# A chunked recurrence inside a decoder layer: its output products take other places in the chunk

## The chip, the cores and the metric

One NeuronCore of one Trainium2 chip runs the whole kernel as one program. The metric is device time in microseconds (us), the median over several executions. The profile is one further execution under the hardware profiler, with its own time.

## What is computed

The reference is one decoder layer over 512 tokens and 1024 channels in float32: two parallel token mixers (an RWKV-7 recurrence with 16 heads of 64, and a three-branch sparse attention), a gated merge, and a gated MLP. The change is inside the recurrence, which per head is

```python
def step(state, inp):
    r_t, w_t, k_t, v_t, a_t, b_t = inp
    sa = jnp.einsum('bhvk,bhk->bhv', state, a_t)
    state = (state * w_t[:, :, None, :] + sa[..., None] * b_t[:, :, None, :]
             + v_t[..., None] * k_t[:, :, None, :])
    return state, jnp.einsum('bhvk,bhk->bhv', state, r_t)
```

run over the 512 tokens. Its results y are normalised per head, scaled by a gate and projected later.

## The kernel before, in words

The kernel does not step token by token. It cuts the 512 tokens into 8 chunks of 64 and works on 8 heads at once: a group has GP = 4 pairs of heads, and there are two groups, so the recurrence runs twice, once per group. Heads of a pair are named h = 0, 1 and lie in partitions 0 to 63 and 64 to 127; pairs of a group are named i.

Per group and chunk c the function `recur` (lines 666 to 798) does the following, each product being of 64 by 64 outputs:

1. xw (lines 760 to 763), for c > 0: the old state St against part 0 of AR. 8 products with 64 rows of contraction, shape 64x64 on TensorE. They go to columns 0 to 255 of the PSUM bank `xw`.
2. W (line 765): VectorE adds LV to xw. GpSimd prepares the decayed state SD meanwhile (line 770).
3. `outputs` of the chunk before (lines 721 to 736, called at 774), explained below.
4. TT (lines 775 to 778): TT times W, 8 products of shape 64x64, to columns 256 to 511 of `xw` and `xs`. VectorE (line 779) and ScalarE (line 780) copy the two halves to UV.
5. A `yield`, then xs (lines 784 to 787): 8 products of BKT with UV, 128 rows of contraction and 64 output partitions, shape 128x64. Line 791 (793 for c = 0) adds SD and gives the next state. Another `yield`.

`outputs(c)` computes y for chunk c: "carried" products of part 1 of AR with the state at the chunk's start (lines 727 to 730, shape 64x64, 8 products, none for c = 0), and "inner" products of GS with UV (lines 731 to 733, shape 128x64, 8 products) that add to the same PSUM sums. It is called one chunk late, between W and TT of chunk c + 1. Its order is by quarters: four carried, four inner, four carried, four inner. In each (head, pair) the carried product opens the sum with start=True and the inner product closes it. The sums live in two PSUM banks `y`, one for each h; one half of the columns of a bank holds two chunks, an even and an odd one, in opposite halves of the partitions. After an odd chunk ScalarE copies the finished half bank to YT (line 736, one instruction for each h). The two banks are allocated anew at c = 0 and c = 4, from a tag with two buffers, so chunk 4 takes over the banks of chunks 0 to 3.

In chunks 3 to 7 the statistics of finished chunk pairs run beside this (`stat1`, `stat2`, lines 741 to 750): a sum on VectorE (743), a scaling (744), a subtraction on GpSimd (745), a square on ScalarE (747), a second sum on VectorE (750).

What fills the waits: a driver interleaves this generator with projection steps (`proj_steps`, lines 286 to 293, each step three 128x512 matmuls at lines 290 to 292 with a shape of 128x128). About one such step is placed in program order at each `yield`. A list scheduler then builds the queues: an instruction that is ready goes by its place in the program, and one that is not ready lets later ones pass. Engines run their queues in order. In the first group the fill is the gate projections and the inputs of head pair 4 (`r`, `v` in the profile), then the preparation of pair 4 (`prep`, lines 495 to 557); in the second it is the query projections (`q`).

After the first group come `finish` (lines 800 to 844) and the preparation of the second group's four pairs; after the second come `finish` again and the attention, whose tables `dist`, `cdist` and `cmask` (lines 945 to 950) are loaded into memory that the recurrence has freed.

Of the kernel before, what the change touches and what calls it, by code (L numbers as in the profile page):

```python
# [32 lines left out]
GP = 4  # L33
# [9 lines left out]
def hybrid_layer(ctx: ExitStack, tc: tile.TileContext, a, out, dbg=None, stop=None):  # L43
    nc = tc.nc
    te, ve, sc, po, sy = nc.tensor, nc.vector, nc.scalar, nc.gpsimd, nc.sync
# [15 lines left out]
    def px(name):  # L61
        return ps.tile([128, 512], F32, tag="px", name=name, bufs=2)

    def py(name):
        return ps.tile([128, 512], F32, tag="py", name=name, bufs=2)
# [63 lines left out]
    def evict(i):  # L129
        last[i.ins.engine] = i  # L130
        return i

    def behind(i):
        tc.add_manual_dep(i.ins, last[i.ins.engine].ins.name,
                          mybir.DependencyInfo(mybir.DependencyClass.NoSync, mybir.DependencyReason.DATA),
                          reason="behind the last eviction")
        return i
# [528 lines left out]
    def recur(gr, g):  # L666
        x1 = gr.x1
        TT = gr.TT
        XN = x1[:, 0].rearrange("p c u -> p u c")
        M2 = x1[:, 0].rearrange("p (i c) t -> p i c t", c=8)  # L670
        L2 = x1[:, 1].rearrange("p (i c) t -> p i c t", c=8)
        yield
        gi = "p (i c j) -> p i c j"
        for q in range(GP // 2):
            pt = px(f"mt{g}{q}")
            ptv = pt.rearrange(gi, i=2, j=32)
            for i in range(2):
                for c in range(8):
                    for h in range(2):
                        lo, up = slice(64 * h, 64 * h + 32), slice(64 * h + 32, 64 * h + 64)  # L680
                        m = te.matmul(ptv[up, i, c], L2[lo, 2 * q + i, c], XN[lo, 16 * q + 8 * i + c], start=True,
                                      stop=True)
                        if q + i + c + h == 0:
                            tc.keep_in_program_order(m)
                yield
                yield
            for h in range(2):
                up = slice(64 * h + 32, 64 * h + 64)
                if h == 0:
                    act_m = sc.activation(M2[up, 2 * q:2 * q + 2], ptv[up], AF.Copy)  # L690
                else:
                    ve.tensor_copy(M2[up, 2 * q:2 * q + 2], ptv[up])
        evict(act_m)
        for h in range(2):
            lo = slice(64 * h, 64 * h + 32)
            behind(sc.activation(gr.diag[0][lo, :, 0:32], gr.diag[1][lo], AF.Copy))
        yield
        for q in range(GP // 2):
            pm = px(f"mm{g}{q}")
            pmv = pm.rearrange(gi, i=2, j=32)  # L700
            for i in range(2):
                for c in range(8):
                    for h in range(2):
                        lo, up = slice(64 * h, 64 * h + 32), slice(64 * h + 32, 64 * h + 64)
                        te.matmul(pmv[lo, i, c], M2[up, 2 * q + i, c], TT[up, 2 * q + i, c, 32:64], start=True,
                                  stop=True)
                yield
                yield
            for h in range(2):
                lo = slice(64 * h, 64 * h + 32)  # L710
                if h == 0:
                    sc.activation(TT[lo, 2 * q:2 * q + 2, :, 32:64], pmv[lo], AF.Copy)
                else:
                    ve.tensor_copy(TT[lo, 2 * q:2 * q + 2, :, 32:64], pmv[lo])
        YT = gr.YT = rh_.tile([128, 4, GP, 2, 64], F32, tag="XB", name=f"YT{g}", bufs=2)
        yield
        hs = [slice(0, 64), slice(64, 128)]
        iv = "p (i v) -> p i v"
        yps = [None]

        def outputs(c, Sc):
            if c % 4 == 0:
                yps[0] = [py(f"y{g}{c}{h}").rearrange("p (a i v) -> p a i v", i=GP, v=64) for h in range(2)]
            y = [b[:, c // 2 % 2] for b in yps[0]]
            for q in range(GP // 2):
                four = [(0, 2 * q), (1, 2 * q + 1), (0, 2 * q + 1), (1, 2 * q)]
                if c:
                    for h, i in four:
                        te.matmul(y[h][hs[(c + i) % 2], i], gr.AR[i][hs[h], 1, c * 64:(c + 1) * 64], Sc[hs[h], i],
                                  start=True, stop=False)  # L730
                for h, i in sorted(four):
                    te.matmul(y[h][hs[(c + i) % 2], i], gr.GS[:, 1 + i, c, h, :], gr.UV[:, c, i, h, :],
                              start=c == 0, stop=True)
            if c % 2:
                for h in range(2):
                    sc.activation(YT[:, c // 2, :, h], y[h], AF.Copy)

        st = gr.st = rh_.tile([128, 2, 4, 2 * GP], F32, tag="gst", name=f"gst{g}", bufs=1)
        sq = gr.sq = {}

        def stat1(a, keep):
            Y8 = YT[:, a].rearrange("p i h v -> p (i h) v")
            keep(ve.tensor_reduce(st[:, 0, a], Y8, axis=AX.X, op=OP.add))
            ve.tensor_scalar(st[:, 0, a], st[:, 0, a], 1.0 / 64, None, op0=OP.mult)
            po.tensor_tensor(Y8, Y8, st[:, 0, a, :, None].to_broadcast([128, 2 * GP, 64]), op=OP.subtract)
            sq[a] = rh_.tile([128, 2 * GP, 64], F32, tag="TB", name=f"SQ{g}{a}", bufs=1)
            sc.activation(sq[a], Y8, AF.Square)

        def stat2(a, keep):
            keep(ve.tensor_reduce(st[:, 1, a], sq[a], axis=AX.X, op=OP.add))  # L750

        def free(i):
            return i

        St = None
        prev = None
        for c in range(8):
            xw, xs = px(f"xw{g}{c}"), px(f"xs{g}{c}")
            if c:
                for i in range(GP):  # L760
                    for h in range(2):
                        te.matmul(xw[hs[h], i * 64:i * 64 + 64], gr.AR[i][hs[h], 0, c * 64:(c + 1) * 64],
                                  St[hs[h], i], start=True, stop=True)
                W = rh_.tile([128, GP, 64], F32, tag="W", name=f"W{g}{c}", bufs=1)
                ve.tensor_tensor(W, xw[:, 0:64 * GP].rearrange(iv, v=64), gr.LV[:, :, c, :], op=OP.add)
                if c >= 3:
                    (stat2 if c % 2 == 0 else stat1)((c - 3) // 2, tc.keep_in_program_order)
                if c < 7:
                    SD = rh_.tile([128, GP, 64], F32, tag="SD", name=f"SD{g}{c}", bufs=1)
                    po.tensor_tensor(SD, St, gr.Dc[:, :, c, None].to_broadcast([128, GP, 64]), op=OP.mult)  # L770
            else:
                W = gr.LV[:, :, 0, :]
            if prev:
                outputs(*prev)
            for i in range(GP):
                for h in range(2):
                    te.matmul((xw, xs)[h][0:64, 256 + i * 64:320 + i * 64], TT[hs[h], i, c, :], W[hs[h], i], start=True,
                              stop=True)
            ve.tensor_copy(gr.UV[0:64, c, :, 0, :], xw[0:64, 256:512].rearrange(iv, v=64))
            sc.activation(gr.UV[0:64, c, :, 1, :], xs[0:64, 256:512].rearrange(iv, v=64), AF.Copy)  # L780
            yield
            prev = c, St
            if c < 7:
                for i in range(GP):
                    for h in range(2):
                        te.matmul(xs[hs[h], i * 64:i * 64 + 64], gr.BKT[i][:, c, hs[h]], gr.UV[:, c, i, h, :],
                                  start=True, stop=True)
                SN = rh_.tile([128, GP, 64], F32, tag="S", name=f"S{g}{c + 1}", bufs=2)
                xsv = xs[:, 0:64 * GP].rearrange(iv, v=64)
                if c:  # L790
                    ve.tensor_tensor(SN, xsv, SD, op=OP.add)
                else:
                    ve.tensor_copy(SN, xsv)
                St = SN
                yield
        outputs(*prev)
        stat2(2, free)
        stat1(3, free)

# [57 lines left out]
    def core(g):  # L857
        return spawn(invert(G[g], g), 0, 1.0), spawn(recur(G[g], g), RD[g], RR[g])
# [646 lines left out]
```

## Time and profile before

| what | value |
|---|---|
| median of 3 runs | 1210.08 us (1209.62 to 1210.79) |
| profiled execution, its time | 1209.59 us |
| profiled execution, span first to last instruction | 1207.8 us |
| TensorE busy | 1174.6 us |
| VectorE, ScalarE, GpSimd busy | 584.6, 582.8, 587.8 us |
| first recurrence, first TT product to last y product | 248.66 to 284.48 us |
| second recurrence | 466.54 to 503.85 us |

In the lines of a profile PE is TensorE's matmul side, PEld its weight loads, DVE is VectorE, ACT ScalarE, POOL GpSimd, and SP the engine that issues most DMAs. A line of the timeline gives start, duration, engine, source line, operation, output<-inputs, the operand form (contraction*output partitions, then the moving operand), a count, and in brackets the idle time before it and what ended it. Each float32 product of the recurrence is two matmul instructions in the trace, so 8 products show as x16. Matmuls overlap in the array, so what a block of them costs is read from the difference between its start and the start of what follows, not from the durations.

### The profile page before, as it was taken

The numbers are of one execution on the slowest core, as the hardware profiler recorded it, in microseconds if no ns is written. First come the engines' busy times: TensorE is split into PE (matmuls) and PEld (weight loads), VectorE is DVE, ScalarE is ACT, GpSimd is POOL, SyncE is SP. The second block draws the span as 40 slices with busy tenths as digits, with TensorE's granted clock in tenths as the row PEclk, the third lists the DMA queues.
The fourth block names the chain that finished last, engine by engine and source line by source line (L and its number), as shares of the span: only waits on it lengthen the run. The fifth ranks groups of instructions, "written<-read, shape, count | busy, mean of one in ns | idle before, by whom it ended". The sixth has DMA issues, their size and how long they took to land.

```text
span 1207.8 us, 19849 instructions
## 1 busy us (share of the span) xinstructions
PE 1174.6 (97%) x7414; PEld 934.0 (77%) x7414; DVE 584.6 (48%) x1196; ACT 582.8 (48%) x1141; POOL 587.8 (49%) x529
## 2 busy tenths in 40 slices
PE   8999999999999999989999999999999999999997
PEld 6888878777777887767666666888888888888886
DVE  4226555436465463476687774855343333431103
ACT  5446653436565334476665664544444444443311
POOL 4336654344565443465466652531366555554440
PEclk8999999999899999999999999999999999999999
DMA  6522335310343543345332214761133333334421
GB/s 220 136 73 81 92 94 166 124 50 22 104 119 103 157 141 115 109 149 184 105 105 71 71 46 127 229 212 37 50 98 92 101 96 97 96 97 131 132 70 70
DMA packets 95651, 131.95 MB, mean 109 GB/s; under 512 B 34177, under 2 KB 37057, under 8 KB 95298
## 3 DMA queue, kind: packets, MB, share of 16 engines
q1 hardware_dynamic: 79634, 116.26, 32.0%
q10 hardware_dynamic: 15920, 14.42, 3.7%
q8 instruction: 58, 0.95, 0.3%
q14 instruction: 39, 0.32, 0.1%
HBM read 108.30 MB, written 19.14 MB: 106 GB/s over the span
## 4 chain that ended last, share of the span: by engine, by line
PE 82%; DVE 7%; ACT 3%; issue 3%; POOL 2%; DMA 2%; SPq 0%; DVEq 0%; POOLq 0%; ACTq 0%
PE pu L212 6%; PE pu L213 6%; PE pu L214 6%; PE dn L1238 3%; PE dn L1236 3%; PE dn L1237 3%; PE o L1080 3%; PE pt L140 3%; PE ub L1132 2%; PE ub L1133 2%; PE ub L1134 2%; PE v L290 2%; PE v L292 2%; PE v L291 2%; PE gt L292 2%
## 5 line engine op out<-in xcount | busy, mean ns | idle before, releaser
L1051 ACT ACTIVATE p<-p,stt 128x384 f32<-128x384 f32 (+3 forms) x128 | 70.9, 555 | 55.7 <-DVE stt L1049 55.4
L1027 POOL TENSOR_SCALAR p<-p,stt 128x512 f32<-128x512 f32 (+1 forms) x64 | 74.1, 1167 | 33.5 <-DVE stt L1022 24.8
L1376 DVE SCALAR_TENSOR_TENSOR u<-pu,cvec,u 128x511 f32<-128x511 f32 x44 | 33.0, 750 | 101.7 <-ACT u L1375 101.7
L1049 DVE CUSTOM_DVE_ANT_0 p<-s,rh 128x384 f32<-128x384 f32 (+3 forms) x128 | 58.4, 484 | 27.9 <-PE s L1044 18.8
L1080 PE MATMUL o<-PT,vt 128*64 128x384 f32 (+3 forms) x256 | 50.5, 451 | 1.1 <-DVE PT L1101 1.1
L140 PE MATMUL pt<-ident,p 128*128 128x128 f32 x320 | 49.6, 276 | 0.0
L1380 POOL TENSOR_TENSOR u<-u,u 128x512 f32<-128x512 f32 x22 | 28.3, 1288 | 38.3 <-DVE u L1377 37.4
L140 PEld LDWEIGHTS pt<-ident,p 128*128 128x128 f32 x320 | 40.1, 142 | 8.4 <-issue 0.4
L1382 DVE TENSOR_TENSOR al<-u,ah 128x512 fp32r<-128x512 f32 x22 | 23.8, 1080 | 45.4 <-ACT ah L1381 45.4
L1044 PE MATMUL s<-kst,qs 128*128 128x512 f32 (+1 forms) x128 | 37.5, 392 | 1.4 <-DVE stt L1049 1.0
L1375 ACT ACTIVATE u<-pu,cvec 128x512 f32<-128x512 f32 x44 | 33.6, 764 | 5.0 <-PE pu L1340 5.0
L1027 DVE TENSOR_SCALAR p<-p,stt 128x512 f32<-128x512 f32 (+1 forms) x64 | 35.0, 581 | 0.9
L1099 ACT ACTIVATE PT<-pt 128x512 f32<-128x512 f32 x48 | 27.9, 582 | 13.5 <-PE pt L140 11.3
L1377 DVE SCALAR_TENSOR_TENSOR u<-pu,cvec,u 128x510 f32<-128x510 f32 x44 | 32.9, 749 | 1.6
L1080 PEld LDWEIGHTS o<-PT,vt 128*64 128x64 f32 x256 | 16.7, 136 | 20.2 <-issue 14.5
L1101 DVE COPY PT<-pt 128x512 f32<-128x512 f32 x32 | 22.0, 686 | 19.2 <-PE pt L140 19.1
L1044 PEld LDWEIGHTS s<-kst,qs 128*128 128x128 f32 x128 | 23.0, 193 | 8.2 <-DVE stt L1049 2.7
L1284 DVE TENSOR_TENSOR p2tm<-dn,gb 128x512 f32<-128x512 f32 x4 | 2.8, 692 | 51.2 <-ACT p2jl L1282 51.2
L587 PEld LDWEIGHTS g<-AR,KB 64*128 64x128 f32 x256 | 20.0, 189 | 9.7 <-DVE GS L590 3.9
L587 PE MATMUL g<-AR,KB 64*128 64x128 f32 x256 | 23.3, 290 | 3.5 <-DVE AR L549 2.8
L1381 ACT ACTIVATE ah<-u 128x512 fp32r<-128x512 f32 x22 | 13.9, 633 | 22.0 <-POOL u L1380 22.0
L1051 ACT ACTIVATION_READ_ACCUMULATOR p<-p,stt 128x1 f32 x128 | 24.0, 188 | 0.0
(1756 smaller groups left out, 3967.3 us busy)
## 6 DMA issues: line engine op xcount, KB each, us to landing
gtd<-gt ACTq DMA_DIRECT2D x16, 256.0 KB, 2.2
qs<-qd SPq DMA_DIRECT2D x32, 128.0 KB, 2.9
g<-gtd SPq DMA_DIRECT2D x16, 256.0 KB, 3.3
xt<-in_x_dram SPq DMA_DIRECT2D x4, 512.0 KB, 5.8
bvd<-bv SPq DMA_DIRECT2D x8, 256.0 KB, 2.1
bvl<-bvd SPq DMA_DIRECT2D x8, 256.0 KB, 2.7
oad<-y SPq DMA_DIRECT2D x8, 256.0 KB, 2.8
kst<-kst ACTq DMA_DIRECT2D x16, 128.0 KB, 3.3
```

Source lines behind the costliest of these rows:

```text
L140: return te.transpose(o, i, ident)
L212: te.matmul(p, wh(k), mh(k), start=first and k == 0, stop=False)
L213: te.matmul(p, wh(k), ml(k), start=False, stop=False)
L214: te.matmul(p, wl(k), mh(k), start=False, stop=last and k == n - 1)
L292: te.matmul(p, wl(k), hh[:, k, :], start=False, stop=k == KT - 1)
L587: te.matmul(gh[h][:, j * 128:(j + 1) * 128], KB[hs, c].rearrange("p s t -> p (s t)"), AR[hs, :, c * 64:(c + 1) * 64], start=True, stop=True)
L1027: (po if b else ve).tensor_scalar(o.pe[e, b, k], o.pe[e, b, k], st[e][:, 3, i:i + 1], None, op0=OP.mult)
L1044: te.matmul(s_[:, :n], qt, kt[:, x, b, :n], start=x == 0, stop=x == 1)
L1049: ve.tensor_tensor_reduce(sb, parts[b], rh[e][:, (3 - qb) * 128:], -1.0, BIG, OP.add, OP.min, st[e][:, 0, i:i + 1])
L1051: sc.activation(sb, sb, AF.Exp, scale=-1.0, bias=st[e][:, 0, i:i + 1], accum_out=st[e][:, 1, i:i + 1])
L1080: te.matmul(acc[e * 64:e * 64 + 64, j * 128:], vt[:, j, b * 256 + g * 64:b * 256 + g * 64 + 64], m[e][:, c:c + n], start=False, stop=last)
L1236: te.matmul(acc[half, t], sh[:, k, tsl], wh[kk], start=k == 0, stop=False)
```

## The change

`outputs` is split into `carried` and `inner`. `carried(c)` stands directly behind the xw products of the same chunk (behind the TT products for c = 4); `inner(c)` stands behind the xs products and the state update of the same chunk. Each is now one uninterrupted list of 8 products. All eight carried sums are open before the first inner product. Only pairs i = 0, 1 open a sum with start=True and only i = 2, 3 close it: pairs i and i + 2 lie in the same partitions of one bank half and now share one start and one stop. Nothing of what is computed changes, nor the number of products.

```diff
-        def outputs(c, Sc):
+        quads = [(h, 2 * q + (h ^ x)) for q in range(GP // 2) for x in range(2) for h in range(2)]
+
+        def ybank(c):
             if c % 4 == 0:
                 yps[0] = [py(f"y{g}{c}{h}").rearrange("p (a i v) -> p a i v", i=GP, v=64) for h in range(2)]
-            y = [b[:, c // 2 % 2] for b in yps[0]]
-            for q in range(GP // 2):
-                four = [(0, 2 * q), (1, 2 * q + 1), (0, 2 * q + 1), (1, 2 * q)]
-                if c:
-                    for h, i in four:
-                        te.matmul(y[h][hs[(c + i) % 2], i], gr.AR[i][hs[h], 1, c * 64:(c + 1) * 64], Sc[hs[h], i],
-                                  start=True, stop=False)
-                for h, i in sorted(four):
+            return [b[:, c // 2 % 2] for b in yps[0]]
+
+        def carried(c, Sc):
+            y = ybank(c)
+            for h, i in quads:
+                te.matmul(y[h][hs[(c + i) % 2], i], gr.AR[i][hs[h], 1, c * 64:(c + 1) * 64], Sc[hs[h], i],
+                          start=i < 2, stop=False)
+
+        def inner(c):
+            y = ybank(c) if c == 0 else [b[:, c // 2 % 2] for b in yps[0]]
+            for h in range(2):
+                for i in range(GP):
                     te.matmul(y[h][hs[(c + i) % 2], i], gr.GS[:, 1 + i, c, h, :], gr.UV[:, c, i, h, :],
-                              start=c == 0, stop=True)
+                              start=c == 0, stop=c == 0 or i >= 2)
...
                         te.matmul(xw[hs[h], i * 64:i * 64 + 64], gr.AR[i][hs[h], 0, c * 64:(c + 1) * 64],
                                   St[hs[h], i], start=True, stop=True)
+                if c != 4:
+                    carried(c, St)
...
-            if prev:
-                outputs(*prev)
             for i in range(GP):
                 for h in range(2):
                     te.matmul((xw, xs)[h][0:64, 256 + i * 64:320 + i * 64], TT[hs[h], i, c, :], W[hs[h], i], start=True,
                               stop=True)
+            if c == 4:
+                carried(c, St)
...
-            prev = c, St
...
                 St = SN
+            inner(c)
+            if c < 7:
                 yield
-        outputs(*prev)
```

More of the change, by code (lines that the diff above doesn't have):

```diff
@@ L755, in recur @@
         St = None
-        prev = None
         for c in range(8):
```

## The prediction

> **What bounds the kernel now.** I read the page first: busy shares, slices, chain.
>
> ```profile
> span 1207.8 us, 19849 instructions
> PE 1174.6 (97%) x7414; PEld 934.0 (77%) x7414; DVE 584.6 (48%) x1196; ACT 582.8 (48%) x1141; POOL 587.8 (49%) x529
> PEclk8999999999899999999999999999999999999999
> PE 82%; DVE 7%; ACT 3%; issue 3%; POOL 2%; DMA 2%; SPq 0%; DVEq 0%; POOLq 0%; ACTq 0%
> ```
>
> TensorE is the bound: busy 97% of the span, 82% of the chain that ended last. The other engines are half idle. Next, the stretches of the two recurrences, as busy time of each engine:
>
> ```profile
> core 0: us, PE busy (x) PEld busy (x) DVE busy (x) ACT busy (x) POOL busy (x), PEclk, DMA share, GB/s
> 248.66:284.48 35.82, 35.27 (x633) 26.48 (x632) 14.45 (x33) 11.23 (x25) 13.79 (x17) 1.00 0.12 37
> 466.54:503.85 37.31, 36.59 (x640) 27.32 (x639) 14.43 (x33) 10.59 (x25) 14.23 (x16) 1.00 0.26 82
> ```
>
> Both are full: PE idles 0.55 and 0.72 us, the clock is at 1.00. So inside them only two things can give time: less work on PE, or those short stalls. The number of products stays. What can shrink is what a block of products costs beside its products, so I went to the timeline of PE. Chunks 0 and 1 of the first group:
>
> ```profile
> 250.17 0.69 PE L786 MATMUL xs<-UV,BKT 128*64 128x64 f32 x16
> 250.68 0.64 PE L732 MATMUL y<-UV,GS 128*64 128x64 f32 x16
> 251.25 0.49 PE L290 MATMUL r<-hh,r4h 128*128 128x512 f32 x1
> 251.68 0.68 PE L762 MATMUL xw<-S,AR 64*64 64x64 f32 x16
> 252.29 0.50 PE L291 MATMUL r<-hl,r4h 128*128 128x512 f32 x1
> ```
>
> And a regular later chunk:
>
> ```profile
> 268.81 0.69 PE L786 MATMUL xs<-UV,BKT 128*64 128x64 f32 x16
> 269.43 0.50 PE L290 MATMUL v<-hh,v4h 128*128 128x512 f32 x1
> 269.76 0.39 PE L291 MATMUL v<-hl,v4h 128*128 128x512 f32 x1
> 270.00 0.40 PE L292 MATMUL v<-hh,v4l 128*128 128x512 f32 x1
> 270.32 0.62 PE L762 MATMUL xw<-S,AR 64*64 64x64 f32 x14
> ...
> 271.05 0.45 PE L732 MATMUL y<-UV,GS 128*64 128x64 f32 x8
> 271.43 0.34 PE L729 MATMUL y<-S,AR 64*64 64x64 f32 x8
> 271.71 0.45 PE L732 MATMUL y<-UV,GS 128*64 128x64 f32 x8
> 272.09 0.27 PE L777 MATMUL xw<-W,TT 64*64 64x64 f32 x1
> ...
> 272.70 0.50 PE L290 MATMUL v<-hh,v4h 128*128 128x512 f32 x1
> ```
>
> Read start to start, a change of operand form costs time on its own. A fill matmul among its like takes 0.24 us (269.76 to 270.00), one alone between two narrow blocks 0.43 (251.25 to 251.68): a filler block that is split off costs 0.43 - 0.23 = 0.20. The xs block alone takes 0.62 (268.81 to 269.43); xs and the inner products behind it, in the same form, take 1.08 (250.17 to 251.25): inner adds 0.46 there. The xw block alone takes 0.61 (251.68 to 252.29); with eight carried instructions among it, rows left out, it takes 0.73 (270.32 to 271.05): eight add 0.12. As blocks of their own, the two halves of inner cost 0.38 each (271.05, 271.71), and the second half of carried 0.28 (271.43).
>
> **The change, part by part.** *Removed in a regular chunk*: three blocks between W and TT, 0.38 + 0.28 + 0.38 = 1.04 us. *Added*: the second half of carried in the xw block, 0.12 (the first half is there already, only of another chunk); inner behind xs, 0.46. *Moved*: the blocks removed were the cover of the wait for W. In chunk 1, where they had run earlier, fill matmuls stand between xw and TT from 252.29 on. Eight carried instructions more don't cover all of it, so I expect one fill matmul there, a third split-off block: 0.20. The fill matmuls themselves are work that has to be done anyway. Net 1.04 - 0.12 - 0.46 - 0.20 = 0.26 us a chunk. Carried products exist in chunks 1 to 7 of two groups: 14 x 0.26 = 3.6 us. Chunk 4 has its carried products behind TT instead, also 64x64, also merged: the same price.
>
> In some chunks the y products are cut up further:
>
> ```profile
> 254.45 0.33 PE L729 MATMUL y<-S,AR 64*64 64x64 f32 x4
> 254.71 0.69 PE L786 MATMUL xs<-UV,BKT 128*64 128x64 f32 x16
> 255.33 0.33 PE L729 MATMUL y<-S,AR 64*64 64x64 f32 x4
> ```
>
> ```profile
> 483.36 0.33 PE L729 MATMUL y<-S,AR 64*64 64x64 f32 x4
> 483.93 0.69 PE L786 MATMUL xs<-UV,BKT 128*64 128x64 f32 x16 [0.24 <-ACT UV L780]
> 484.55 0.33 PE L729 MATMUL y<-S,AR 64*64 64x64 f32 x4
> ```
>
> Each group has one such place: two blocks of four at 0.26 (254.45 to 254.71) where eight merged cost 0.12. That is 0.40 each, 0.8 us together. The last chunks are cut up too; I put nothing on that, and it is a reason for the low end.
>
> *Stalls.* PE waits before xs for ScalarE's half of UV:
>
> ```profile
> L786 PE MATMUL xs<-UV,BKT 128*64 128x64 f32 x224 | 9.6, 228 | 1.3 <-ACT UV L780 1.3
> ```
>
> ```profile
> 273.50 0.63 ACT L747 ACTIVATE SQ<-YT 128x512 f32<-128x512 f32 x1 [5.05 <-POOL YT L745]
> 274.03 0.36 ACT L780 ACTIVATE UV<-xs 64x256 f32<-64x256 f32 x1
> ```
>
> The 1.3 us are chunks in which the square (L747), which waits for GpSimd, stands ahead of the UV copy on ScalarE; TT had ended at 272.70. With the three y blocks gone, TT follows W sooner, while GpSimd's part still starts from W. So UV tends to be ready first and to be queued first. Bounds: all 1.3 gained, or as much lost in chunks that are free of it now. I take a gain of 0.6, nearer to half.
>
> *A new wait.* Carried of chunks 2 and 6 writes the other half of bank columns that ScalarE is still copying out (L736) for chunks 1 and 5; before, it came a whole chunk later. Queued behind it on PE stand TT and the fill; W's successor TT, UV and xs wait for that.
>
> ```profile
> 257.14 0.66 ACT L736 ACTIVATE YT<-y 128x256 f32<-128x256 f32 x2 [1.56 <-PE y L732]
> 285.95 1.28 ACT L520 ACT_TABLE_LOAD   x1
> ```
>
> The two copies take 0.66 us from the end of inner. Carried comes after about two fill matmuls (0.43 + 0.23) and xw (0.61): 1.27 us. If ScalarE is free, 0.6 us are left over and the cost is nothing; if it has just begun another 0.63 us instruction, almost nothing; with a table load in the way up to 0.66 + 1.28 - 1.27 = 0.7 at each of four places, 2.7 us. I take 0.3 in all, near the lower end, because the ScalarE rows of both recurrences hold no table load. [...]
>
> *The copies to YT* (0.66 us on ScalarE after odd chunks) move from the gap before UV to the gap before W; ScalarE was idle 1.56 us before them, so that is free. No DMA moves, and SP's and POOL's own instructions keep their order.
>
> Sum: 3.6 + 0.8 + 0.6 - 0.3 = 4.7 us.
>
> **Does it reach the end?** After the first group:
>
> ```profile
> 284.10 1.22 DVE C L508
> 298.40 2.61 DVE YT L810 x2
> ```
>
> ```profile
> 295.00:300.00 5.00, 3.29 (x23) 2.22 (x22) 5.00 (x9) 2.90 (x5) 2.88 (x2) 0.87 0.06 5
> ```
>
> From 284 to 300 the chain runs through VectorE: the preparation of the next pair (C) and the scaling of the finished group (L810). C hangs on matmuls that ran as fill in the last chunks, L810 on the last y sums. Both move forward with the recurrence. PE idles here, so a shift is passed on whole if both move, and not at all if something else sets this stretch. After the second group the waits of the DMA queue show the link:
>
> ```profile
> SPq L946 <- PE y L732: 2.8, 1, 2.8
> ```
>
> The attention's first table waited 2.8 us for the last inner products. So I pass the sum on. The profiled execution took 1209.59 us: 1209.59 - 4.7 = 1204.9. It lies 0.49 us under the median of the runs (1210.08), so for the median I say 1205.4.
>
> **The rivals.**
> *More than that.* If no fill matmul is put between carried and TT, 0.20 is not paid 14 times: 2.8 us more, 1202.6; with the rest of the stalls (0.7) and some 0.4 for the cut-up last chunks 1201.5. For it: carried takes 0.24 us in all and could nearly cover W. Against: chunk 1's row of fill there.
> *Saved and lost again after the recurrence.* The time between 284 and 310 or from 504 on is set by VectorE, GpSimd or DMA that don't move, or the list scheduler reorders the start of the attention. Then the end stays within 2.4 us: 1208 to 1212, say 1209. For it: PE idles 1.71 us from 295 to 300 alone. A form of it is that the change does not do what it says, because the scheduler pulls the groups apart again (1210.1). Against: the chunk 0 row, where xs and inner did stay together.
> *Slower: carried waits on ScalarE at the head of PE's queue.* The place is chunks 2 and 6, four times. If the copies are queued behind a table load and two other instructions, carried is late by 0.66 + 1.28 + 2 x 0.63 - 1.27 = 1.93 us each time: 7.7 us against the 5.0 gained without it, 1212.8. It decides from 1.25 us late on (nothing gained), and is over 0.2% slower from 1.85. Against: no table load stands in those stretches.
>
> **How the numbers follow.** 0.2%, 2.4 us, is about what a measurement can tell from no change. The forecast case, 1203 to 1207.6: 0.54. More: 0.13. Saved and lost, or pulled apart: 0.20. Slower by the wait: 0.08, and 0.05 for other new orders of the queues that end slower. So faster 0.67, same 0.20, slower 0.13. The range leaves out most of the slower case and the tail of the gain: 1201.5 to 1210.9.
>
> **What would show it.** In the timeline: xw x16 with carried x16 directly behind, one fill matmul, TT, about three, xs x16 with inner x16 as one block of about 1.08 us, two fill matmuls. The windows of the recurrences at 33.2 and 34.9 us for the same fill (before 35.8 and 37.3). The idle before L786 put down to UV below 1.3 us. The table's wait on y shorter, with a DMA issue some 4 us earlier. I am wrong if idle before carried is put down to the YT copies, if the y products still stand in blocks of eight, or if the windows shrink and the time does not.

## The result and the profile after

| | before | after |
|---|---|---|
| median of the runs | 1210.43 us (1209.62 to 1212.47) | 1202.06 us (1201.39 to 1202.32) |
| profiled execution, span | 1207.8 us | 1200.0 us |
| ratio, 95% interval | | 0.9929 [0.9917, 0.9941] |

The kernel is 8.4 us faster by the medians, 7.8 by the profiled spans; the forecast was 4.7. Two executions further down took far longer, 6448 us of the changed kernel (without it its median of 1201.48 there is 1201.18) and 2899 us of the kernel before, and stand in no ratio. The lines of the profile's page that answer to those of before:

```profile
span 1200.0 us, 19851 instructions
PE 1169.2 (97%) x7414; PEld 928.8 (77%) x7414; DVE 583.1 (49%) x1196; ACT 583.3 (49%) x1141; POOL 587.5 (49%) x529
PE 84%; DVE 7%; issue 3%; ACT 3%; POOL 2%; DMA 1%; SPq 0%; DVEq 0%; POOLq 0%; ACTq 0%
```

The same 7414 matmul instructions, and PE is busy 5.4 us less. The windows of the two recurrences, with the columns as before:

```profile
249.05:283.62 34.57, 34.49 (x644) 25.68 (x643) 17.02 (x37) 14.18 (x30) 15.17 (x18) 1.00 0.12 38
461.34:496.98 35.64, 35.61 (x645) 25.94 (x644) 14.35 (x33) 10.69 (x25) 14.19 (x16) 1.00 0.27 83
```

They are 1.25 and 1.67 us shorter and do more: the first now also holds six fill matmuls and five small ones of the preparation (L518), the second four fill matmuls. At 0.23 us a fill matmul and 0.13 a small one (0.83 us of rows for six, start to start 0.76) that is 2.0 and 0.9 us, so at equal fill they gained 3.3 and 2.6 us, 5.9 together. PE idles 0.08 and 0.03 us in them, 0.55 and 0.72 before. A regular chunk in the timeline of PE, lines moved by the change (xw L767, carried L731, TT L782, xs L792, inner L738):

```profile
265.40 0.62 PE L767 MATMUL xw<-S,AR 64*64 64x64 f32 x14
...
265.91 0.40 PE L731 MATMUL y<-S,AR 64*64 64x64 f32 x14
266.24 0.49 PE L290 MATMUL v<-hh,v4h 128*128 128x512 f32 x1
266.67 0.27 PE L782 MATMUL xw<-W,TT 64*64 64x64 f32 x1
...
267.28 0.50 PE L291 MATMUL v<-hl,v4h 128*128 128x512 f32 x1
267.62 0.39 PE L292 MATMUL v<-hh,v4l 128*128 128x512 f32 x1
267.85 0.40 PE L290 MATMUL v<-hh,v4h 128*128 128x512 f32 x1
268.17 0.69 PE L792 MATMUL xs<-UV,BKT 128*64 128x64 f32 x16
268.69 0.64 PE L738 MATMUL y<-UV,GS 128*64 128x64 f32 x16
269.25 0.50 PE L291 MATMUL v<-hl,v4h 128*128 128x512 f32 x1
269.59 0.40 PE L292 MATMUL v<-hh,v4l 128*128 128x512 f32 x1
269.92 0.51 PE L767 MATMUL xw<-S,AR 64*64 64x64 f32 x10
```

This is the order that was forecast, block for block: one fill matmul between carried and TT, three, xs and inner as one block of 1.08 us (268.17 to 269.25), two. From xw to xw it takes 4.52 us (265.40 to 269.92); before, the same products with six fill matmuls took 4.78 (265.54 to 270.32). This chunk is no exception: of the twelve intervals from xw to xw in the two groups, seven hold six fill matmuls, six of these at 4.52 or 4.53 us and one at 4.63. The groups of instructions by form, and the DMA queue's waits:

```profile
L792 PE MATMUL xs<-UV,BKT 128*64 128x64 f32 x224 | 9.6, 228 | 0.1
L731 PE MATMUL y<-S,AR 64*64 64x64 f32 x224 | 8.0, 224 | 0.0
```

```profile
SPq L953 <- PE y L731: 0.5, 1, 0.5
```

PE no longer waits for ScalarE's half of UV before xs (0.1 us idle in all, 1.3 before), and it never waits before carried: the copies to YT are done in time. The first table of the attention waited 2.8 us for the last inner products before; now it waits 0.5 us, and for carried products.

The recurrences explain 5.9 of the 7.8 us. The rest shows between the first TT product of the first recurrence and that of the second, from here on *the stretch*. As windows of PE alone, first before, then after:

```profile
248.66:466.54 217.88, 211.40 (x1837) 0.98 0.35 102
```

```profile
249.05:461.34 212.29, 207.02 (x1838) 0.98 0.35 105
```

That is 5.59 us less. PE idles 217.88 - 211.40 = 6.48 us in the one and 5.27 in the other. PEclk is under 1.00 in both, and cut finer it is not a little slow all the time but at half in a few pieces of equal length:

```profile
295.30:298.70 3.40, 1.69 (x16) 0.99 0.00 0
298.70:302.12 3.42, 3.42 (x16) 0.51 0.40 115
302.12:305.53 3.41, 2.18 (x33) 0.99 0.29 77
305.53:308.94 3.41, 2.91 (x21) 0.50 0.65 163
308.94:312.35 3.41, 3.41 (x11) 0.51 0.22 61
```

```profile
292.56:295.97 3.41, 2.90 (x29) 1.00 0.30 105
295.97:299.38 3.41, 2.07 (x30) 1.00 0.39 117
299.38:302.80 3.42, 2.92 (x21) 0.50 0.33 53
302.80:306.21 3.41, 3.41 (x11) 0.50 0.12 31
306.21:309.62 3.41, 3.41 (x17) 1.00 0.78 269
```

Three such windows of 3.41 us stand behind the first recurrence before, two after; each loses half of itself, 1.71 us. (That is an upper bound: in one window of each kernel PE also idles 0.5 us, which is counted twice, 0.25 us in both.) So the stretch comes apart into three sums:

| first TT of one recurrence to first TT of the next, us | before | after | difference |
|---|---|---|---|
| PE idle | 6.48 | 5.27 | -1.21 |
| lost to half clock | 3 x 1.71 = 5.12 | 2 x 1.71 = 3.41 | -1.71 |
| the rest: PE's work | 206.28 | 203.61 | -2.67 |
| stretch | 217.88 | 212.29 | -5.59 |

From the second start to the end 741.26 us became 738.67, which is -2.59, what the second recurrence gained at equal fill. The first group began 0.39 us later in the profiled execution after; -5.59 - 2.59 + 0.39 = -7.8.

### The profile page after: what moved, and what is told of

It reads as the page before. It is cut to its first block, busy times and chain, and to the rows that moved or that the text cites. A ratio compares the mean times of both kernels' runs of the same rounds, so it can differ in the third digit from the quotient of the medians.

```text
span 1200.0 us, 19851 instructions
## 1 busy us (share of the span) xinstructions
PE 1169.2 (97%) x7414; PEld 928.8 (77%) x7414; DVE 583.1 (49%) x1196; ACT 583.3 (49%) x1141; POOL 587.5 (49%) x529
## 4 chain that ended last, share of the span: by engine, by line
PE 84%; DVE 7%; issue 3%; ACT 3%; POOL 2%; DMA 1%; SPq 0%; DVEq 0%; POOLq 0%; ACTq 0%
PE pu L212 6%; PE pu L214 6%; PE pu L213 6%; PE dn L1245 3%; PE dn L1243 3%; PE dn L1244 3%; PE o L1087 3%; PE pt L140 3%; PE ub L1139 2%; PE ub L1140 2%; PE ub L1141 2%; PE v L290 2%; PE v L291 2%; PE v L292 2%; PE gt L292 2%
```

## The experiments

Ratios are to the kernel before on the same chip. The theories of the first two rounds: **A**, all of the gain is made inside the recurrences and passed on; **B**, that gain and some 2.4 us more, because the preparation of pair 4 now starts under the last chunks.

**One group only.** The new order in the first group, the old one in the second, and the other way round.

```diff
+        new = g == 0
...
-                if c != 4:
+                if c != 4 and new:
                     carried(c, St)
...
+            if prev and not new:
+                outputs(*prev)
```

> New order in the first group's recurrence only, old order in the second. Theory A (only the recurrences pay: fewer changes of operand form and no stalls, 3.3 us at equal fill in the first group, 2.6 in the second): 1210.4 - 3.3 = 1207.1 us. Theory B (besides that, the preparation of head pair 4 ran under the last chunks of the first recurrence, and the stretch behind it, where TensorE idles, got 2.4 us shorter): 1210.4 - 5.7 = 1204.7 us.

> New order in the second group only. Both theories: about 1210.4 - 2.5 = 1207.9 us, and the gains of the two single groups add up to that of both (8.4). Theory A in its strict form needs the larger part here or an even split (4 and 4, 1206.2); theory B needs the smaller part here.

Measured: first group only 1203.12 us, 0.9936 [0.9924, 0.9949], under the figures of both theories; second only 1207.06 us, 0.997 [0.9958, 0.9982], 0.8 us under theirs. The first pays more than twice as much as the second, though its recurrence gained only 0.7 us more. With the first alone the stretch took 211.12 us, 6.8 less than before, with one half-clock window; with the second alone 218.04, as before, with three. By the ratios the two gains add up to 0.94%, 11.4 us, where both orders together gave 0.71%, 8.6 us: they don't add up as both theories had it, though with each ratio known to 0.12% only just, and one window more or less is 1.7 us.

**Regrouped, not moved.** The y products stay one chunk late between W and TT, but as eight carried and eight inner with the shared sums. The edit is to the kernel before; some lines are left out.

```diff
-            for q in range(GP // 2):
-                four = [(0, 2 * q), (1, 2 * q + 1), (0, 2 * q + 1), (1, 2 * q)]
...
+            if c:
+                for h, i in quads:
+                    te.matmul(y[h][hs[(c + i) % 2], i], gr.AR[i][hs[h], 1, c * 64:(c + 1) * 64], Sc[hs[h], i],
+                              start=i < 2, stop=False)
+            for h in range(2):
+                for i in range(GP):
...
```

> The y products stay one chunk late between W and TT, only their order there changes: all eight carried, then all eight inner. 26 changes of operand form fewer than before over both recurrences (46 and 48 against 62 and 58), nothing moved in the chunk; the stalls of TensorE before xs may stay. If the changes of form pay (0.17 us each): 1210.4 - 4.4 = 1206.0 us. If moving the products to other places pays (TT no longer behind them, preparation earlier): 1210 us, no change.

Measured: 1207.48 us, 0.9975 [0.9965, 0.9985], between the two figures and nearer to that of the form changes. The timeline of PE in a regular chunk:

```profile
266.05 0.51 PE L763 MATMUL xw<-S,AR 64*64 64x64 f32 x10
...
266.90 0.69 PE L733 MATMUL y<-UV,GS 128*64 128x64 f32 x16
267.51 0.27 PE L778 MATMUL xw<-W,TT 64*64 64x64 f32 x1
...
270.54 0.62 PE L763 MATMUL xw<-S,AR 64*64 64x64 f32 x14
```

The chunk takes 4.49 us with six fill matmuls, no more than the 4.52 of the changed kernel: inner costs 0.61 by itself here (266.90 to 267.51), but no fill block is split off. So what pays in a regular chunk is the merging. But PE still idles 1.3 us in each recurrence (0.1 or less with the moved products), and behind the first one the 1.85 us that its window lost (33.97 against 35.82) were nearly all given back: the stretch took 217.52 us, with 9.55 us of PE idle and two half-clock windows. For the first group that is the prediction's second rival, saved and lost again, in this kernel and not in the changed one.

**Inner one chunk late.** Carried in its own chunk, but behind the inner products of the chunk before, which stand behind this chunk's xw, W and SD.

```diff
-                if c != 4:
-                    carried(c, St)
...
+            if c:
+                inner(c - 1)
+                if c != 4:
+                    carried(c, St)
...
-            inner(c)
...
+        inner(7)
```

> Carried products in the same chunk as in the changed kernel, inner products still one chunk late, between xw and carried. 53 and 52 changes of form in the two recurrences (before 62 and 58, changed kernel 44 and 46); the preparation of pair 4 starts in the last-but-one chunk, as in the changed kernel. Price of the form changes alone: 15 x 0.17 = 2.6 us, 1207.8 us. With the earlier preparation (2.4 us): 1205.4 us. If the number of form changes is not what counts but the cover: as the changed kernel, 1202 us.

Measured: 1206.23 us, 0.9963 [0.9951, 0.9976], between the figures with and without the earlier preparation; the rival with 1202 us is out. The stretch took 215.42 us, with two half-clock windows. What a change of form costs is best read from chunks with the same 80 matmul instructions of the recurrence, six fill matmuls and no idle time of PE. Before, such a chunk takes 4.78 us with seven changes of form inside it (from 265.54 us), here 4.67 with six (from 265.84), in the changed and the regrouped kernel 4.52 and 4.49 with five, wherever the products stand: about 0.13 us a change.

Over the whole stretch it comes out less evenly. Forms change 53 times within the first recurrence here, 62 times before and 44 after, but PE's work is 205.74 us against 206.28 and 203.61: half of the changes saved, a fifth of the work.

**Preparation held, preparation early.** To test B: the changed kernel with pair 4's first preparation product kept behind the last inner products; the kernel before, and the changed one, with the inputs of pair 4 drawn ahead of two gate projections so that its preparation starts 16 steps earlier.

```diff
-        te.matmul(pw, lh[:, :128], ltw, start=True, stop=False)
+        m = te.matmul(pw, lh[:, :128], ltw, start=True, stop=False)
+        if p == GP:
+            tc.keep_in_program_order(m)
```

```diff
-            fill = itertools.chain(*gates_(NG0), inputs(GP, os_[GP]))
-            drive(fill, *r0, p4 := spawn(later(prep, GP, os_[GP]), 8 * (NG0 + 3) + 1, PA))
+            fill = itertools.chain(*gates_(NG0 - 2), inputs(GP, os_[GP]), *gates_(2))
+            drive(fill, *r0, p4 := spawn(later(prep, GP, os_[GP]), 8 * (NG0 - 2 + 3) + 1, PA))
```

> The changed kernel, with one thing undone: the first matmul of pair 4's preparation keeps its place in the program, behind the last inner products, instead of filling a gap of the last-but-one chunk. The recurrences themselves stay (44 and 46 form changes). Theory B: from that matmul a chain of some 15 us leads to pair 4's first g products, whatever the recurrence does; it starts some 6.5 us later, so the time is 2.4 to 6.6 us above the changed kernel, 0.9950 to 0.9985 of before (1204.5 to 1208.7 us). Theory A: as the changed kernel, 0.993 of before.

> The kernel before, with its old order of y products; only the fill of the first recurrence is reordered, so that two gate projections come behind the inputs of pair 4 and the preparation of pair 4 can start some 16 projection steps earlier. 62 and 58 form changes as before. Theory B: 2.4 us or more faster than before (ratio 0.998 or lower, 1208 us or less). Theory A: no change, 1.000.

> The changed kernel with the same reordered fill. Theory B: the preparation chain is no longer last, what is left of the idle time behind the first recurrence shrinks further: 0 to 3 us under the changed kernel, ratio to before 0.990 to 0.993. Theory A: as the changed kernel, 0.993; the 48 form changes in the first recurrence in place of 44 cost 0.7 us.

Measured: held 1203.28 us, 0.9937 [0.9925, 0.9949]; the kernel before with early preparation 1202.88 us, 0.9941 [0.9929, 0.9954]; the changed one with it 1202.35 us, 0.9929 [0.9913, 0.9946], with runs from 1198.6 to 1204.9. Neither theory stands. B falls by the first run: holding the preparation back costs next to nothing. A falls by the second, where it had no change. The first result has two effects in it that cancel. The windows of PE in the held kernel:

```profile
289.87:293.29 3.42, 2.67 (x12) 1.00 0.00 0
293.29:296.70 3.41, 1.02 (x5) 1.00 0.00 0
296.70:300.11 3.41, 3.41 (x22) 0.50 0.24 81
```

PE's idle time in the stretch rose from 5.27 to 7.21 us, as B says, but it fell into one place, and one half-clock window followed in place of two: +1.9 and -1.7. And the kernel before, with nothing changed in the recurrence but an earlier preparation, lost no window at all: its stretch took 211.71 us, 6.2 less, at the same work (206.44 us). The changed kernel gains nothing from the same edit: in its profile (1204.88 us) the stretch took 214.58 us, with three half-clock windows.

**Carried one chunk late.** Inner behind its own xs, where it opens the sums; carried behind the next chunk's xw, where it closes them. Of the edit only the new place of carried is shown; `copies` holds the copies to YT that stood in `inner`.

```diff
-                if c != 4:
-                    carried(c, St)
+                if prev:
+                    carried(*prev)
+                    copies(prev[0])
...
```

> Inner products behind xs of their chunk as in the changed kernel, but opening the sums; carried products one chunk late, behind the next chunk's xw, closing them. 43 and 46 form changes, preparation of pair 4 in the same gaps as in the changed kernel. If form changes and the place of the preparation are all: as the changed kernel, ratio 0.993 (within 0.001). If it counts that y is finished in its own chunk (copies, statistics, the state's buffer): slower than that by the last chunk's products and more, 0.995 or above.

Measured: 1196.97 us, 0.9889 [0.9874, 0.9904], faster than both expectations. Its recurrences take as long as those of the changed kernel (34.77 and 35.60 us) and PE's work is the same (203.74); its stretch took 206.75 us, with 3.01 us of PE idle and no half-clock window. So the 5.5 us of difference in the stretch lie in what the engines do *behind* the first recurrence.

**What PE waits for there.** The timeline of the changed kernel, some rows left out:

```profile
293.85 0.63 ACT L124 ACTIVATE v5h<-v51r 128x512 fp32r<-128x512 f32 x1 [1.62 <-DMA v51r<-in_wf_dram]
294.29 1.27 DVE L590 TENSOR_TENSOR GS<-g,mask 128x512 f32<-128x512 f32 x2
294.50 1.28 ACT L811 ACT_TABLE_LOAD   x1
...
295.79 0.32 ACT L811 ACTIVATE gst<-gst,vec 128x32 f32<-128x32 f32 x1
...
296.60 2.62 DVE L817 TENSOR_TENSOR YT<-YT,gst 128x512 f32<-128x512 f32 x2
...
297.83 0.66 PE L140 MATMUL gt<-ident,YT 128*128 128x128 f32 x4 [0.45 <-DVE YT L817]
299.15 1.27 DVE L590 TENSOR_TENSOR GS<-g,mask 128x512 f32<-128x512 f32 x2
...
299.88 0.47 PE L603 MATMUL pl<-UV,GS 64*64 64x64 f32 x2 [1.40 <-DVE GS L590]
```

ScalarE stands 1.62 us before a copy of the next weight half (v51r), whose DMA has not landed. Behind it wait the table load and the root of `finish` (L811). When the root is there, VectorE does two scalings of YT (L817, 2.62 us; part of `finish`) ahead of the last two masks GS (L590; part of the preparation of the next pair), and PE waits 1.40 us for those. In the kernel with carried one chunk late the root stands ahead of that copy. **Theory C**: this order on ScalarE decides the idle time and the lost windows. **Theory D**: the order of the y products does. In the one kernel the copy is tied behind the root, in the other the root behind the copy, both with the kernel that they change beside them on the same chip. Lines between are left out.

```diff
-        act(hi, raw, AF.Copy)
+        m = act(hi, raw, AF.Copy)
+        if name in ("v51",):
+            behind(m)
...
-        sc.activation(st[:, 0], st[:, 1], AF.Sqrt, scale=1.0 / 64, bias=epsg)
+        evict(sc.activation(st[:, 0], st[:, 1], AF.Sqrt, scale=1.0 / 64, bias=epsg))
```

```diff
...
+        if name == "v51":
+            tc.add_manual_dep(roots[0].ins, m.ins.name,
+                              mybir.DependencyInfo(mybir.DependencyClass.NoSync, mybir.DependencyReason.DATA),
+                              reason="behind the split")
...
+        roots.append(sc.activation(st[:, 0], st[:, 1], AF.Sqrt, scale=1.0 / 64, bias=epsg))
```

> The changed kernel itself, as the base of two of the three runs beside it. Both theories: 1202 us, 0.993 of before; from the first TT product of the first recurrence to the first TT product of the second 212.3 us, of it 5.3 us with PE idle and two windows of 3.4 us at half clock.

> The changed kernel with one order on ScalarE fixed: behind the first recurrence the table load and the root of the norms of finish come ahead of the copy of v5's second half, which there waits 1.62 us for its DMA. Theory C, that this place on ScalarE decides what is left of PE's idle time and so of the clock behind the first recurrence: the 1.62 us before the root go, PE's idle time in that stretch falls from 5.3 to about 3 us, the half-clock windows from two to none or one (1.7 us lost in each), the stretch from 212.3 to 207 to 209 us, the median to 1196.7 to 1199. Theory D, that the gain behind the recurrence belongs to the order of the y products itself (as in the kernel with carried one chunk late): nothing changes, 1202, 212 us.

> The kernel with inner behind its own xs and carried one chunk late, once more, as the base of the run behind it. Both theories: 1197 us, 0.989 of before, the stretch between the recurrences 206.8 us with 3.0 us of PE idle and the clock at full.

> The kernel with carried one chunk late, with ScalarE's order behind the first recurrence turned to that of the changed kernel: the copy of v5's second half stands ahead of the table load and the root. Theory C: the root comes about 2 us later, PE idles 5 us or more in the stretch in place of 3.0, one to three half-clock windows appear, the stretch grows from 206.8 to 210 to 213 us, the median to 1200 to 1203. Theory D: the order of the y products has made the gain, so the stretch stays within 1 us of 206.8 and the median at 1197 to 1198.

| kernel | median, us | ratio | stretch | PE idle | half-clock windows | PE's work |
|---|---|---|---|---|---|---|
| changed kernel | 1201.48 | 0.9927 [0.9913, 0.994] | 212.14 | 5.38 | 2 | 203.35 |
| the same, root first | 1195.29 | 0.9877 [0.9863, 0.989] | 207.34 | 3.44 | 0 | 203.90 |
| carried one chunk late | 1195.74 | 0.9886 [0.9871, 0.99] | 206.73 | 3.01 | 0 | 203.72 |
| the same, root behind the copy | 1197.76 | 0.9895 [0.988, 0.991] | 208.00 | 3.92 | 0 | 204.08 |

C's first half holds: one dependence on ScalarE, nothing in the recurrence, takes 5.9 us off the changed kernel by the medians (1201.18 to 1195.29) and 6.2 by the profiled spans, and no kernel here is clearly faster (the ratio of the kernel with carried one chunk late lies within its interval); D would have left it where it was. Of the 6.2 us 4.8 lie in the stretch, as C had it. The other 1.5 lie behind the start of the second recurrence (738.68 us to the end became 737.19), which C doesn't explain. The timeline of that kernel (lines moved by two: root L813, masks L592, scalings L819):

```profile
293.07 0.32 ACT L813 ACTIVATE gst<-gst,vec 128x32 f32<-128x32 f32 x1 [0.22 <-DVE gst L812]
293.30 0.62 ACT L124 ACTIVATE v5h<-v51r 128x512 fp32r<-128x512 f32 x1
...
295.02 0.84 DVE L819 TENSOR_TENSOR YT<-YT,gst 128x512 f32<-128x512 f32 x1
295.78 1.28 DVE L592 TENSOR_TENSOR GS<-g,mask 128x512 f32<-128x512 f32 x2
...
296.98 2.22 DVE L819 TENSOR_TENSOR YT<-YT,gst 128x512 f32<-128x512 f32 x3
```

Counted from the start of the recurrence the root comes 2.0 us earlier (293.07 - 248.37 against 295.79 - 249.05), and one scaling, not two, is ahead of the last masks. C's second half missed: the late root cost the other kernel 1.3 us of stretch and 2.0 us of the medians (the intervals of the ratios overlap), not 3 to 6. Here theory D, with a median of 1197 to 1198 and a stretch within 1 us of 206.8, came nearer. The root came at 297.98, 3.8 us later against the start of the recurrence than in the kernel beside it, and yet:

```profile
296.56 0.69 DVE L595 TENSOR_TENSOR GS<-g,mask 128x512 f32<-128x512 f32 x1 [1.04 <-PE g L592]
...
298.34 0.35 DVE L823 RECIPROCAL gst<-gst 128x32 f32<-128x32 f32 x1 [1.09 <-ACT gst L822]
298.61 0.63 DVE L595 TENSOR_TENSOR GS<-g,mask 128x512 f32<-128x512 f32 x1
299.15 2.20 DVE L828 TENSOR_TENSOR YT<-YT,gst 128x512 f32<-128x512 f32 x2
```

With the root that late, the queues were laid out otherwise, and all masks stand ahead of the scalings. From 290 to 310 us PE idled 0.68 us at most in one window, and no window was lost. So a late root is not what costs by itself. Nor does an early one help by itself: in the kernel before it came 44.8 us behind the start of the recurrence, as early as in the kernel with the root first (44.7), and ahead of that copy too, and three windows were lost. There VectorE and PE read:

```profile
298.40 2.61 DVE L810 TENSOR_TENSOR YT<-YT,gst 128x512 f32<-128x512 f32 x2
300.94 1.27 DVE L590 TENSOR_TENSOR GS<-g,mask 128x512 f32<-128x512 f32 x2
...
305.30 1.27 DVE L590 TENSOR_TENSOR GS<-g,mask 128x512 f32<-128x512 f32 x2
306.03 0.47 PE L603 MATMUL pl<-UV,GS 64*64 64x64 f32 x2 [1.73 <-DVE GS L590]
```

Two scalings stand ahead of even the first masks, and two more (left out) ahead of the last. So C is too narrow: as these traces read, ScalarE's order matters by way of VectorE's. The last mask was done 57.9 us behind the start of the recurrence before, 51.4 in the changed kernel, 48.7 with the root first, 47.9 with carried one chunk late, and the stretches fall in the same order: 217.88, 212.29, 207.34, 206.75 us. It isn't the only thing that counts, for the held kernel has the order of before and 55.6 us, yet a stretch of 212.80. What costs is idle time of PE in one place and the half-clock windows that follow: in the five profiles in which PE idled at most 1.03 us in any 3.41 us of the 30 behind the first recurrence no window there was lost, in the nine with 1.69 us or more one to three. All this is read from the traces; no run fixed VectorE's order alone. And the windows are counted in one profiled execution of each kernel, in two of the changed kernel and of the one with carried late, which agreed there.

## Why the prediction was right, and where its sizes were off

*The price of the y products* (4.4 us: 3.6 and 0.8). Right. At equal fill the windows gained 5.9 us, of which 1.16 are idle time (0.55 + 0.72 - 0.08 - 0.03), so PE's work fell by 4.7; the windows come to 32.5 and 34.7 us, forecast were 33.2 and 34.9. The regular chunk gained 4.78 - 4.52 = 0.26, the very figure of the sum, and the fill matmul in the gap was there, which refutes the rival that had none. That the measured 1202.06 us lies where this rival had put it (1201.5 to 1202.6), and under the 1203 to 1207.6 of the forecast case, is luck: what made up the difference lies elsewhere, as the last but one point below shows. It lies within the whole range, 0.6 us above its lower end. What the sum left at nothing, the cut-up last chunks, is the likely rest of 0.3. A simpler account comes near: the regular chunk has two changes of operand form less, at about 0.13 us each, and in the first recurrence the form changes 18 times less in PE's queue while PE's work in the stretch fell by 2.67 us, 0.15 us a change. It does not fit every kernel: the same division gives 0.06 us with inner one chunk late and 0.24 in the changed kernel with early preparation, 0.11 to 0.16 in the others. What takes the time at a change of form no run here shows.

*The stalls* (0.6 of 1.3 us). The mechanism was right, the size too small: all waits of xs for UV went but 0.1, and 1.16 us of idle in all. The bound, all 1.3 gained, was the better value. The regrouped kernel, where the y products still stand between W and TT, kept its stalls (1.3 us in each recurrence).

*The new wait of carried* (0.3 us lost). No run shows this term. In the profile of the changed kernel L731 has no idle time before it (0.0 us), and the copies to YT had ended 0.28 us or more before the carried products of chunks 2 and 6, so whether these would wait for them is not shown either. The slower rival had no place to begin.

*"So I pass the sum on."* Right for the second group, as far as one profile of a kernel can tell: 2.59 us gained in the recurrence, 2.59 at the end. That they agree so closely is luck. With the new second recurrence the time from its start to the end is 737.2 to 739.2 us in six profiles, with the old one 739.6 to 741.3 in the three that have the old order there unchanged; the means differ by 2.1. Wrong for the first: there 3.3 us became 5.6. The step argued that a shift is passed on whole or not at all. It looked at PE's idle time behind the recurrence as fixed, though it quoted the row with a clock of 0.87 in it. That idle time depends on the order in which the list scheduler lays VectorE's and ScalarE's queues out, new orders of the recurrence change it, and with it how many half-clock windows follow. Nor does PE wait longest here for what the step named, C and the scalings: its longest wait is that for the masks, 1.73 us before and 1.40 after, and the last mask came 6.5 us earlier (51.4 us behind the start in place of 57.9), once masks stood ahead of scalings. Here PE's idle time fell by 0.74 us outside the recurrence, and one window of 1.71 us less was lost: 2.45 us, which is what was missing. In the regrouped kernel, whose masks kept the old order, idle time gave back nearly all of the first group's gain (9.55 us idle), so the sign could not be read from the edit.

*Sum.* Forecast 4.4 + 0.6 - 0.3 = 4.7; by the profiles 4.7 + 1.2 + 0 = 5.9 in the recurrences, 2.45 behind, the first group's later start of 0.39 and a rest of 0.1 against it: 7.8.

## What to carry to other kernels

Where PE is full, count the changes of operand form in its queue: merging blocks of the same form paid about 0.13 us a change in a regular chunk, whether the blocks were moved or not. Here a gain in a full stretch was passed on with interest (3.3 us became 5.6) or given back (1.85 became 0.36 in the regrouped kernel) in the next stretch where PE idles; read that stretch in windows of 3.41 us, in which the clock changed here, because idle time in one place cost itself and then up to 1.71 us for every window at half clock. And look there first, at which waiting instruction heads a queue and what stands behind it: one dependence that put a short root ahead of a copy still waiting for its DMA brought 4.8 us in that stretch, more than half of what the whole change brought.

## What was not expected of the hardware

The clock fell to half in whole windows of 3.41 us that lie on a grid of that length: in the traces of the kernel before and of the changed one the 12 and 10 stretches of one clock each begin a whole number of windows of 3.413 us behind the first. In the kernel before, falls followed windows in which PE was busy 1.69 and 2.18 us, in the changed one 2.07, in the held one 1.02; none followed the held kernel's window with 2.67 busy. The border is not sharp: in the same two traces, up to PE's last matmul, nine falls followed windows with 0.45 to 2.24 us of idle (the two with less than 1.0 in the first 10 us of the kernel), and windows with up to 1.72 stayed at full clock. The grid does not start with the kernel: its first border lies 1.70 us behind the span's start before, 2.43 after and 3.15 in the held kernel, so which idle time falls together into one window is in part chance.
